# Four mixer layers and two feed-forwards on one core: the builder's context orders the instructions by its timeline simulation

## The chip, the cores and the metric

One core of one Trainium2 chip runs the kernel. The metric is the device time of one execution in microseconds. Of the kernel before there are three runs, 1022.75 to 1022.98 us, median 1022.92. The core's engines have streams of their own and run side by side: TensorE (PE in the profile, its weight loads PEld), VectorE (DVE), ScalarE (ACT), GpSimd (POOL) and the queue that issues transfers (SP).

## The reference

The input is 256 tokens of width 1024. Two blocks work on them. The first has two equal layers, each on a normalised `h`:

```python
(hq, hf, hi, hgo, hz, nq, kcm, vcm, ksl, vsl, kwn, vwn, ngate, nz) = split(rmsnorm(h) @ w_in[i])
y_hg  = rmsnorm(hgrn2_chunkwise(hq, log_f, k_hg, hi)) * sigmoid(hgo) * silu(hz)
kc    = rmsnorm(compress(kcm));  vc = compress(vcm)        # 15 compressed keys and values
o_nsa = gates[0] * o_cmp + gates[1] * o_slc + gates[2] * o_win
y_nsa = o_nsa * silu(nz)
h = h + concat([y_hg, y_nsa]) @ w_out[i]
h = h + sigmoid(rmsnorm(h) @ w_pg[i]) * (p[i] @ w_pp[i])
```

`hgrn2_chunkwise` is a gated linear recurrence over four heads, `o_cmp`, `o_slc` and `o_win` are eight-head softmax attentions over compressed, selected and windowed keys. The second block has an even layer (a recurrence and short convolutions), a feed-forward, an odd layer and another feed-forward, each added to `h`, with a norm at the end. The odd layer joins a spatial gating unit (gelu of a projection, normalised, mixed over tokens) and an eight-head softmax attention with a decay. A feed-forward is `(silu(gate) * val) @ w_down`, where gate and val come from a three-tap convolution of `x @ w_up` (2 x 2816 columns).

## The kernel before

The residual `h` is held in SBUF as two tiles of 128 tokens, and each layer works on all 256 tokens. Weights pass through once, in pieces of 128 x 1024. `wload` and `wgroup` issue the transfer of a piece (`raw`, three buffers); ScalarE makes the rounded part (`whi`, L262), VectorE the rest (`wlo`, L265), five buffers each. A product is three matmuls: high by high, high by low, low by high (`mm3`, L364). Helpers hold most instructions, so their lines repeat: L257 transfer, L262 ScalarE operation, L265 VectorE operation of two tensors, L364 matmul, L411 POOL.

`first_layer` (L566 to 815) does the first block's layers. From `h` it makes the normalised and transposed `xA` (`xT`, L430), then the projections: `F`, `hq`, `K`, `Q` (the queries `nq`), `hz`, `hgo` and `nz`. Between them run the recurrence, head by head, and from L719 on the queries' norm and transposes (`qT`). The compressed keys come from `compress` (L864 to 895): matmul `pkc`, its squares on ScalarE (`ksq`), sums on VectorE (`kv`), a root on POOL (`kr`), scaling on VectorE (`kc`), a transpose on TensorE (`kcT`). Scores `cs` (L364) give the weights `ce`, transposed as `cpt`.

`nsa` (L980 to 1031) does the selected and windowed attention in twelve blocks per layer, four for the first half of tokens and eight for the second. A block is: four or two matmuls `as` and a mask matmul `causal` into one of two accumulators; on VectorE the negated maximum `anm` (L1017); on ScalarE the exps `pr` with their sums; on VectorE the reciprocal (L1024), the gate and the multiplication of `pr` by `af`; on TensorE four transposes `apt` (L1030); on VectorE the copy `pts` (L1031). Two blocks' copies feed `no`. After the gate `yA` the output matmuls `po` add into `h`. `pp` is the product of `p` and `w_pp`, `pg` the gate of that last step.

In the odd layer `as`, `pr` and `fo` belong to the attention, `og` (gate side) and `ou` (other side) to the spatial gating. In a feed-forward `up` is the first product, `pd` the second, with four sums (two halves of tokens by two halves of columns). The last norm (`Last`, L494, L498) writes `fin`, which goes out by four transfers.

No table sets the order of instructions, and it isn't written by hand. `body` emits operations as the text has them, and the builder's context collects them, simulates when each could start, and puts out each engine's and queue's stream in the order which that simulation gives. Engines run their streams in that order; waits on other engines are put in by the context.

## Time and profile before

| what | value |
|---|---|
| median of three runs | 1022.92 us (1022.75 to 1022.98) |
| the profiled execution's own time | 1022.92 us |
| its span, first to last instruction | 1021.1 us |
| TensorE busy | 985.7 us, 97% of the span |
| TensorE weight loads | 869.6 us, 85% |
| VectorE busy | 806.4 us, 79% |
| ScalarE busy | 599.1 us, 59% |
| POOL busy | 35.3 us, 3% |
| read from memory | 164.30 MB, 162 GB/s over the span |
| chain that ended last | TensorE 74%, VectorE 10%, transfers 6%, ScalarE 4% |

The busy share says which engine has the most work, the chain which engine the end waited for, and the table by stretches whether this holds in each stage. A row of a timeline gives start, duration, engine, line, operation, output and inputs, and in brackets how long the engine had stood idle and what ended it. Matmuls overlap in TensorE's pipe, so the step from start to start is shorter than a single one's duration.

### The profile page before, as it was taken

What the parts mean: (1) busy time and instruction counts of PE and PEld (TensorE: products, weight loads), DVE (VectorE), ACT (ScalarE), POOL (GpSimd) and SP (SyncE); (2) the same over time, 40 slices, a digit from 0 to 9 for tenths busy, and PEclk for the clock granted to TensorE, in tenths of its full rate; (3) what the DMA queues carried; (4) which work ended last, traced back from release to release, by engine and by line L of the source; (5) the groups of instructions that cost most, each with busy time, mean ns of one, the idle gap of its engine ahead of it and who ended that gap; (6) DMA issues with size and microseconds to landing.
All of it is one profiled execution on the core that took longest, in us unless ns stands there. A gap on an engine that the chain in (4) does not pass through costs nothing.

```text
span 1021.1 us, 17129 instructions
## 1 busy us (share of the span) xinstructions
PE 985.7 (97%) x6524; PEld 869.6 (85%) x6524; DVE 806.4 (79%) x1439; ACT 599.1 (59%) x1061; POOL 35.3 (3%) x44
## 2 busy tenths in 40 slices
PE   7999899999998999999999999999989999999997
PEld 5879787778797786799889999998888899999995
DVE  5778889987878898778968877777667869777776
ACT  6753555577644654666657555555756556555553
POOL 1001100000002000000100000000000000000000
PEclk9999999999999999999999999999999999999999
DMA  8741543565503525555755766665582546666661
GB/s 295 240 145 53 146 147 115 192 197 157 186 15 112 179 63 174 169 164 160 236 181 150 222 186 186 186 186 177 166 227 62 175 143 203 186 186 188 186 186 57
DMA packets 48098, 168.03 MB, mean 165 GB/s; under 512 B 5648, under 2 KB 6672, under 8 KB 47376
## 3 DMA queue, kind: packets, MB, share of 16 engines
q1 hardware_dynamic: 48016, 166.94, 53.7%
q8 instruction: 51, 0.84, 0.3%
q14 instruction: 31, 0.25, 0.1%
HBM read 164.30 MB, written 1.05 MB: 162 GB/s over the span
## 4 chain that ended last, share of the span: by engine, by line
PE 74%; DVE 10%; DMA 6%; ACT 4%; issue 3%; POOL 2%; SPq 0%; POOLq 0%; ACTq 0%; DVEq 0%
PE up L364 25%; PE pd L364 12%; PE po L364 5%; DVE wlo L265 4%; PE pg L364 3%; PE pl L364 2%; PE hq L364 2%; PE nz L364 2%; PE hgo L364 2%; PE Q L364 2%; ACT whi L262 2%; PE as L364 2%; PE F L364 2%; DMA raw<-in_win_dram 2%; POOL hr L411 2%
## 5 line engine op out<-in xcount | busy, mean ns | idle before, releaser
L262 ACT ACTIVATE whi<-raw 128x1024 fp32r<-128x1024 f32 (+2 forms) x295 | 309.7, 1052 | 231.6 <-PE up L364 59.8
L265 DVE TENSOR_TENSOR wlo<-raw,whi 128x1024 fp32r<-128x1024 f32 (+2 forms) x295 | 356.8, 1212 | 91.9 <-ACT whi L262 88.8
L364 PE MATMUL pd<-whi,fhl 128*128 128x512 f32 x352 | 115.8, 391 | 0.0
L364 PE MATMUL up<-xFlo,whi 128*128 128x256 f32 x352 | 99.6, 283 | 0.5 <-DVE xFlo L435 0.5
L364 PE MATMUL up<-xDlo,whi 128*128 128x256 f32 x352 | 99.6, 283 | 0.5 <-DVE xDlo L435 0.5
L364 PE MATMUL up<-xDhi,whi 128*128 128x256 f32 x352 | 99.4, 283 | 0.2 <-ACT xDhi L262 0.2
L364 PE MATMUL up<-xFhi,whi 128*128 128x256 f32 x352 | 99.4, 283 | 0.2 <-ACT xFhi L262 0.2
L364 PE MATMUL up<-xFhi,wlo 128*128 128x256 f32 x352 | 99.5, 283 | 0.0
L364 PE MATMUL up<-xDhi,wlo 128*128 128x256 f32 x352 | 99.5, 283 | 0.0
L364 PEld LDWEIGHTS pd<-whi,fhl 128*128 128x128 f32 x352 | 66.2, 188 | 14.0 <-ACT fhl L262 0.9
L1047 DVE SCALAR_TENSOR_TENSOR fc<-fp,colp,fc 128x255 f32<-128x255 f32 (+1 forms) x176 | 73.5, 478 | 0.8 <-ACT fc L262 0.7
L364 PE MATMUL pd<-wlo,fhl 128*128 128x512 f32 x176 | 69.1, 392 | 0.0
L364 PEld LDWEIGHTS up<-xDlo,whi 128*128 128x128 f32 x352 | 67.5, 192 | 1.5 <-DVE xDlo L435 0.7
L364 PEld LDWEIGHTS up<-xFlo,whi 128*128 128x128 f32 x352 | 67.5, 192 | 1.5 <-DVE xFlo L435 0.7
L364 PEld LDWEIGHTS up<-xFhi,whi 128*128 128x128 f32 x352 | 67.3, 192 | 1.2 <-ACT xFhi L262 0.5
L364 PEld LDWEIGHTS up<-xDhi,whi 128*128 128x128 f32 x352 | 67.3, 192 | 1.2 <-ACT xDhi L262 0.5
L364 PEld LDWEIGHTS up<-xFhi,wlo 128*128 128x128 f32 x352 | 67.5, 192 | 0.0
L364 PEld LDWEIGHTS up<-xDhi,wlo 128*128 128x128 f32 x352 | 67.5, 192 | 0.0
L262 ACT ACTIVATE fc<-fp,colp 128x256 f32<-128x256 f32 x88 | 47.6, 586 | 2.5 <-DVE fp L265 2.4
L262 ACT ACTIVATE fhl<-fc 128x256 fp32r<-128x256 f32 x44 | 18.2, 414 | 44.9 <-DVE fc L265 44.9
L262 ACT ACTIVATE pr<-as,anm 128x128 f32<-128x128 f32 (+1 forms) x80 | 32.6, 423 | 17.8 <-PE apt L1030 6.7
L265 DVE TENSOR_TENSOR fp<-up,R 128x512 f32<-128x512 f32 x44 | 30.3, 690 | 15.9 <-PE up L364 15.8
(477 smaller groups left out, 2416.2 us busy)
## 6 DMA issues: line engine op xcount, KB each, us to landing
raw<-in_up_dram SPq DMA_DIRECT2D x88, 512.0 KB, 3.9
raw<-in_win_dram SPq DMA_DIRECT2D x64, 512.0 KB, 4.3
raw<-in_down_dram SPq DMA_DIRECT2D x44, 512.0 KB, 4.1
raw<-in_ein_dram SPq DMA_DIRECT2D x20, 512.0 KB, 4.1
raw<-in_oin_dram SPq DMA_DIRECT2D x20, 512.0 KB, 4.2
raw<-in_wout_dram SPq DMA_DIRECT2D x16, 512.0 KB, 3.7
raw<-in_wpg_dram SPq DMA_DIRECT2D x16, 512.0 KB, 4.0
cw<-in_cw_dram SPq DMA_DIRECT2D x4, 1024.0 KB, 6.9
```

The lines of the kernel that those rows point to most:

```text
L262: A.activation(o, i, f, **kw)
L265: V.tensor_tensor(o, x, y, op=op)
L364: PE.matmul(o, l, r, start=start, stop=stop)
L411: G.tensor_tensor(o, v, mh[:, :v.shape[1]], op=OP.pow)
L1047: V.scalar_tensor_tensor(dst[:, k:], src[:, :T - k], w, dst[:, k:], op0=OP.mult, op1=OP.add)
```

## The change

One argument is given to the builder's context. The operations, tiles and buffers are as they were; the simulation by which the streams are ordered is another.

```diff
     out = nc.dram_tensor("out_0_dram", (T, D), F32, kind="ExternalOutput").ap()
-    with tile.TileContext(nc) as tc:
+    with tile.TileContext(nc, schedule_with_timeline_sim=True) as tc:
         body(tc, aps, offs, out)
```

TensorE keeps its 6188 instructions and VectorE its 1441, SP and POOL theirs; ScalarE has 951 instead of 945, six more loads of an activation table. What moves is shown at three places.

TensorE, layer 0, in the attention blocks. `as_1317` is the third block of the layer, `apt` the transposes of earlier blocks. Before:

```order
L364 MATMUL nz_1693<-xA0hi_93,wlo_1697 128x256
L364 MATMUL nz_1693<-xA0hi_93,whi_1696 128x256
L364 MATMUL as_1317<-kA_412,qs_1131 128x2x128
L364 MATMUL as_1317<-kA_413,qs_1131 128x2x128
L364 MATMUL as_1317<-kA_412,qs_1131 128x2x128
L364 MATMUL as_1317<-kA_413,qs_1131 128x2x128
L364 LDWEIGHTS identb_82
L364 MATMUL as_1317<-causal_81,identb_82 128x512
L364 MATMUL no_1224<-ces_1245,VB_1202 128x512
L1030 MATMUL apt_1267<-ident_76,pr_1258 128x128 x4
L364 MATMUL nz_1693<-xA0lo_94,whi_1696 128x256
L364 MATMUL nz_1693<-xA0hi_93,wlo_1697 128x256
```

TensorE of the same layer with the change, from the start of the compressed keys on:

```order
L729 MATMUL qT_1180<-ident_76,q2_1170 128x128 x4
L364 MATMUL pkc_1186<-cw2_651,hT_649 32x64
L364 MATMUL pvc_1200<-cw2_651,rep_1198 128x64
L890 MATMUL kcT_1216<-ident_76,kc_1195 128x32
L364 MATMUL as_1273<-kA_412,qs_1131 128x2x128
L364 MATMUL as_1273<-kA_413,qs_1131 128x2x128
L364 MATMUL as_1273<-kA_412,qs_1131 128x2x128
L364 MATMUL as_1273<-kA_413,qs_1131 128x2x128
L364 LDWEIGHTS identb_82
L364 MATMUL as_1273<-causal_81,identb_82 128x512
L364 MATMUL cs_1225<-kcT_1218,qnT_945 128x32 x4
L364 MATMUL as_1295<-kA_412,qs_1131 128x2x128
```

And further on, at `as_1317`:

```order
L364 MATMUL as_1317<-kA_412,qs_1131 128x2x128
L364 MATMUL as_1317<-kA_413,qs_1131 128x2x128
L364 LDWEIGHTS identb_82
L364 MATMUL as_1317<-causal_81,identb_82 128x512
L364 MATMUL no_1224<-ces_1245,VB_1202 128x512
L1030 MATMUL apt_1267<-ident_76,pr_1258 128x128 x4
L1030 MATMUL apt_1289<-ident_76,pr_1280 128x128 x4
L364 MATMUL as_1370<-kA_412,qs_1173 128x512
```

Before, `hgo`, `nz` and `pp` matmuls stood between the links of the chain and between the blocks. With the change 48 `hgo`, 96 `nz`, 24 `pp` and 24 `po` stand ahead of `pkc`, and 42 `po` between the blocks; layer 1 has the same pattern.

ScalarE, odd layer, at the end of the attention blocks. Before:

```order
L262 ACTIVATE pr_8255,asum_8192<-as_8246,anm_8193 128x256 x2
L262 ACTIVATE pr_8277,asum_8192<-as_8268,anm_8193 128x256 x2
L262 ACTIVATE whi_8524<-raw_8522 128x1024
L262 ACT_TABLE_LOAD
L262 ACTIVATE og_8377<-og0_8327,r_7741 128x512
L262 ACTIVATE og_8400<-og1_8328,r_7741 128x512
L262 ACTIVATE yEhi_8116<-fo_8191 128x4x128
L262 ACTIVATE sq_8379<-og_8377 128x512
```

With the change:

```order
L262 ACTIVATE whi_8524<-raw_8522 128x1024
L262 ACT_TABLE_LOAD
L262 ACTIVATE pr_8136,asum_8119<-as_8121,anm_8120 128x128 x4
L262 ACT_TABLE_LOAD
L262 ACTIVATE og_8377<-og0_8327,r_7741 128x512
L262 ACT_TABLE_LOAD
L262 ACTIVATE pr_8166,asum_8119<-as_8151,anm_8120 128x128 x4
L262 ACT_TABLE_LOAD
L262 ACTIVATE og_8400<-og1_8328,r_7741 128x512
```

The gelus of `og` moved between the exps of the attention, with a load at each turn from one function to the other.

SP, the start of the program, behind the last transfer of `h`. Before:

```order
L257 DMA raw<-in_win_dram 128x1024
L257 DMA colp<-in_colp_dram 128x889
L257 DMA rowp<-in_rowp_dram 128x512
L257 DMA raw<-in_win_dram 128x1024 x2
L257 DMA stage<-in_c_stage_dram 128x2048
L257 DMA causraw<-in_c_causal_dram 128x128
L257 DMA raw<-in_win_dram 128x1024 x3
L257 DMA cw_651<-in_cw_dram 128x128
L257 DMA cw_653<-in_cw_dram 128x2048
```

With the change:

```order
L257 DMA colp<-in_colp_dram 128x889
L257 DMA rowp<-in_rowp_dram 128x512
L257 DMA stage<-in_c_stage_dram 128x2048
L257 DMA causraw<-in_c_causal_dram 128x128
L257 DMA cw_651<-in_cw_dram 128x128
L257 DMA cw_653<-in_cw_dram 128x2048
L257 DMA raw<-in_win_dram 128x1024 x3
L257 DMA cw_674<-in_cw_dram 128x2048
```

The weight pieces `raw` moved behind the constants and behind two pieces of the compression's weights (`cw`). At the end of the program the last matmuls of the four `pd` sums alternate, where each sum was finished before the next one.

## Rows read from the trace of the kernel before

**Rows 1.** The page, busy time and share of the span by engine.
```profile
PE 985.7 (97%) x6524; PEld 869.6 (85%) x6524; DVE 806.4 (79%) x1439; ACT 599.1 (59%) x1061; POOL 35.3 (3%) x44
```
**Rows 2.** Busy time by stretch: length, each engine's (instructions), granted clock, DMA share, GB/s.
```profile
0.00:25.00 25.00, 18.15 (x77) 14.40 (x78) 13.55 (x31) 16.43 (x34) 2.99 (x14) 1.00 0.87 295
...
62.00:113.00 51.00, 49.38 (x395) 43.69 (x394) 39.63 (x98) 22.78 (x40) 6.35 (x4) 1.00 0.24 71
...
135.00:181.00 46.00, 44.55 (x280) 34.38 (x279) 43.06 (x97) 28.99 (x85) 0.27 (x3) 1.00 0.34 110
...
535.00:706.00 171.00, 171.00 (x1233) 162.17 (x1232) 137.62 (x210) 99.64 (x146) 0.00 (x0) 1.00 0.63 185
...
730.00:797.00 67.00, 60.95 (x485) 54.87 (x485) 46.30 (x70) 40.20 (x74) 4.43 (x3) 1.00 0.53 152
...
831.00:1002.00 171.00, 171.00 (x1230) 162.16 (x1231) 137.68 (x211) 99.51 (x146) 0.00 (x0) 1.00 0.61 179
1002.00:1021.10 19.10, 11.78 (x53) 9.11 (x52) 10.44 (x22) 6.27 (x14) 1.10 (x2) 0.90 0.14 55
```
**Rows 3.** The chain that ended last, layer 0: start, duration, what.
```profile
132.17 5.79 PE hgo L364 x25
...
152.64 3.42 PE nz L364 x27
```
**Rows 4.** Tiles of layer 0: duration min/median/max in ns, first and last start in us.
```profile
L364 PE MATMUL Q<-whi,xA0hi x16: 387/396/502, 62.2 to 94.5; 128*128 128x512 f32 x16
...
L1017 DVE TENSOR_REDUCE anm<-as x12: 659/682/691, 135.3 to 169.8; 128x2 f32<-128x512 f32 x8, 128x4 f32<-128x512 f32 x4
...
L1031 DVE COPY pts<-apt x12: 679/688/692, 141.5 to 180.3; 128x512 f32<-128x512 f32 x12
...
L364 PE MATMUL po<-whi,yAlo x32: 387/389/497, 176.6 to 201.8; 128*128 128x512 f32 x32
```
**Rows 5.** Timeline of layer 0, compressed keys and first block.
```profile
124.05 0.30 PE L364 MATMUL pkc<-cw,hT 128*32 128x64 f32 x2
...
130.11 0.24 PE L890 MATMUL kcT<-ident,kc 32*128 32x32 f32 x1
...
135.33 0.68 DVE L1017 TENSOR_REDUCE anm<-as 128x4 f32<-128x512 f32 x1
```
**Rows 6.** VectorE's groups by form, 108 to 205 us: busy us, mean ns, idle before.
```profile
L265 DVE TENSOR_TENSOR wlo<-raw,whi 128x1024 fp32r<-128x1024 f32 x25 | 30.2, 1216 | 2.6 <-ACT whi L262 2.6
L265 DVE TENSOR_TENSOR pr<-pr,af 128x512 f32<-128x512 f32 x12 | 8.2, 682 | 0.0
...
L265 DVE TENSOR_TENSOR h<-po,h 128x512 f32<-128x512 f32 x4 | 2.7, 672 | 0.6 <-PE po L364 0.6
```
**Rows 7.** Start: SP's timeline, and busy time by stretch.
```profile
9.02 0.33 SPq L257 DMA_DIRECT2D raw<-in_win_dram  x1
...
17.00:21.00 4.00, 4.00 (x21) 3.24 (x20) 3.25 (x10) 3.15 (x6) 0.15 (x1) 1.00 0.98 331
```
**Rows 8.** ScalarE's timeline in the odd layer.
```profile
735.62 1.28 ACT L262 ACT_TABLE_LOAD   x1
736.92 0.42 ACT L262 ACTIVATE fe<-fe 8x256 f32<-8x256 f32 x1
```
**Rows 9.** The end: timeline, and busy time by stretch.
```profile
1013.22 5.08 SPq L257 DMA_DIRECT2D out_dram<-fin  x4
...
1015.35 0.69 DVE L265 TENSOR_TENSOR fin<-h,gfin 128x512 f32<-128x512 f32 x1 [0.24 <-DMA out_dram<-fin]
...
1014.50:1017.00 2.50, 0.00 (x0) 0.00 (x0) 1.56 (x6) 0.85 (x5) 0.55 (x1) 1.00 0.38 144
1017.00:1021.10 4.10, 0.00 (x0) 0.00 (x0) 0.46 (x1) 0.70 (x1) 0.00 (x0) 0.54 0.34 128
```
**Rows 10.** The chain that ended last, start of the program.
```profile
9.47 3.35 PE F L364 x7
...
17.47 5.99 PE F L364 x26
```

## Prediction, made before the result

> **What bounds the kernel now.** I read the engine totals first, then the busy time by stretch, then the tile rows of layer 0, and last single instructions. TensorE is busy 985.7 of 1021.1 us [rows 1], so at most 35.4 us is idle there. Both feed-forward stretches of 171 us are full to the last hundredth, 171.00 of 171 [rows 2]; VectorE has 137.62 and 137.68 in them and waits for TensorE. Those 342 us only give or take time if TensorE's own work changes, and it doesn't: both orders have the same matmuls. The other limit is in layers 0 and 1: while the selected-attention blocks run (135 to 181 us) VectorE is busy 43.06 of 46 and TensorE 44.55 [rows 2]. There a chain with many hands (matmul, VectorE maximum, ScalarE exp, VectorE scale, transposes, VectorE copy) runs beside dense projections that need no one's answer. Those projections keep TensorE at work while the chain turns. So the question is which matmuls stand beside the chain after the change.
>
> **Layers 0 and 1.** In the new order 48 `hgo`, 96 `nz`, 24 `pp` and the first 24 of 96 `po` matmuls stand ahead of `pkc`, the matmul that starts the compressed-key chain; before they stood behind it. Of `po` 42 more lie between the blocks; nothing else dense does. Price: 512 columns cost 5.79/25 = 0.232 us, the 256 columns of `nz` 3.42/27 = 0.127 us [rows 3]. So 96 x 0.232 + 96 x 0.127 = 34.5 us of cover goes ahead.
>
> The stretch from the first `Q` matmul (62.2) to the end of the last `po` (201.8 + 0.39 = 202.2) takes 140.0 us [rows 4]. For the new order I add it up anew:
> - First `Q` to `pkc`: 124.05 - 62.2 = 61.9 us before [rows 4, 5], plus 34.5, makes 96.4. TensorE idles about 1.6 us of 62 to 113 [rows 2], which the dense work standing ready could fill, and I take half as much again for 113 to 124: 96.4 - 2.4 = 94.0.
> - `pkc` to the first maximum `anm`: 135.33 - 124.05 = 11.3 us [rows 5]. The chain passes ScalarE, VectorE, POOL and VectorE before `kcT`, then goes on through `cs`. Until now `hgo` matmuls covered it. In the new order `kcT` stands directly behind `pvc`, so TensorE waits for it in order: 11.3 us bare.
> - First `anm` to the last copy `pts`: 45.7 us now (135.3 to 180.3 + 0.69) [rows 4]. VectorE must do per block a maximum, a copy [rows 4] and a multiply [rows 6], 0.682 + 0.688 + 0.682 = 2.05 us, 24.6 us for twelve blocks. TensorE's part is larger: of its 44.55 us there [rows 2] 92 `nz`, 24 `pp`, 12 `po` and some 13 `hgo` (until 137.96 [rows 3]) leave, 11.7 + 5.6 + 2.8 + 3.0 = 23.1, and 42 `po` come, 9.7: 31.2 us, the lower end. The weight subtractions between the blocks' steps (1.216 us each [rows 6]) move ahead, so 45.7 is the upper end. Only two accumulators serve the blocks and each engine waits for the other's answer, so I take 38, in the middle.
> - Last copy to last `po`: 30 `po` are left, 7.0 us, and the last outputs still have to be gated and transposed; by the present wait between copy 180.3 and the yet open `po` I give that 3.6 us: 10.6.
>
> 94.0 + 11.3 + 38 + 10.6 = 153.9 against 140.0: **+14 us per layer, +28 for two** (the second has the same order). With 31.2 the layer gives +7.1, with 45.7 it gives +21.6; both ends go into the range.
>
> VectorE's subtractions for that dense work must be done earlier too. VectorE has room, 39.63 us busy of 51 from 62 to 113 [rows 2]; I take nothing for them, and a lack of it is in the upper end.
>
> **Start.** SP now issues `colp`, `rowp`, `stage`, `causraw` and two of the `cw` transfers ahead of the fourth `raw` chunk, issued at 9.02 before [rows 7]. Together that is about 2.9 MB by shapes. At the 331 GB/s of 17 to 21 us [rows 7] these take 8.9 us and the chunk itself 1.6, so it lands near 20 and after two passes of about 1.2 us, copy and subtraction [rows 6], feeds `F` from 22.4 on; `F`'s last quarter (12 x 0.232 = 2.8) then ends at 25.2 instead of 23.5 [rows 10]. **+1.7 us**, between 0 (the bytes have to come anyway) and 4.
>
> **ScalarE in the odd layer.** Exp and gelu now alternate between the attention blocks, and the whole program has 21 table loads instead of 15. One takes 1.28 us; the next instruction begins at 736.92, 0.02 us after the load's end (735.62 + 1.28) [rows 8]. So 6 x 1.28 = 7.7 us more on ScalarE. TensorE idles 6 of the 67 us from 730 to 797 [rows 2]; in the new order `og` and `ou` matmuls stand between the blocks and can cover these idle times, while the exps wait for tables. I set both against each other: **0**, from -4 to +7.7. The Trainium skill (ScalarE: Activation LUTs, "What ACT_TABLE_LOAD costs") adds a drain and calls each switch about 2.66 us, an estimate of 16 us for six. By that page the sum would be 8 us higher; the rows here show the load alone and no drain behind it, so I keep 1.28.
>
> **Joints and tail.** Where the first feed-forward hands over to the odd layer, and that one to the second feed-forward, the sums now finish together instead of one after another, so the next normalisation starts later. The nearest row is the add into `h`, 0.672 us each [rows 6], three behind the first: **+2** at each joint (0 to 3). At the end of the kernel likewise: the four `pd` sums were finished one by one, and the first half's output went out from 1013.22 [rows 9]; now all four end within some 12 matmuls. VectorE then has four adds and four multiplies left (8 x about 0.69 = 5.5 us) where 1.56 + 0.46 = 2.0 us lay behind the last matmul, and the fourth `fin` buffer waits for an output transfer, which cost 0.24 us before [rows 9]. **+4**, from +2 to +6. Even layer and feed-forward: 0; their TensorE rows keep their pattern, and a full TensorE covers the rest.
>
> **Sum.** 28 + 1.7 + 0 + 2 + 2 + 4 = 37.7. The profiled execution took 1022.92 us, its span 1021.1 and 1.8 around it, and it is the median itself. 1022.9 + 37.7 = 1060.6, say **1061 us**. Lower ends together give 14 + 0 - 4 + 0 + 2 = 12, so 1035; upper ends 43 + 4 + 7.7 + 6 + 6 = 67, so 1090. All at one end at once is unlikely; half of the way to each gives 1048 to 1075.
>
> **Rivals.**
> *Faster, about 1008 (0.08).* Work standing ready earlier fills TensorE's idle time. Of its 35.4 us [rows 1] start and tail hold 14 (6.9 of the first 25 us, 7.3 of the last 19.1) [rows 2]; of the other 21 two thirds recovered is 14, so 1022.9 - 14 = 1009, and 1 less where the start gains as well. It decides at 35.4 us: if block stretch and chain together (45.7 + 11.3 now, the chain covered) take less than that, a layer falls below 140.0. For it: VectorE is freed exactly there, and TensorE's own part is only 31.2. Against it: the chain stands in TensorE's row with nothing of other kind between its links.
>
> *Nearly nothing, about 1027 (0.10).* With no subtractions and gates in the way every hand answers at once: the blocks run at TensorE's 31.2 us, and the chain takes its bare instructions; three of them take 0.30, 0.24 and 0.68 us [rows 5], so for the dozen I estimate 5.6, half of 11.3. A layer then costs 94.0 + 5.6 + 31.2 + 10.6 = 141.4, +1.4; the odd layer gains its 4, the joints cost nothing, start and tail 5.7: 1022.9 + 2.8 - 4 + 5.7 = 1027. VectorE's 43.06 of 46 speaks for it, since subtractions are what made that stretch full.
>
> *Much slower by the clock, about 1110 (0.04).* Seven 512-column matmuls of `F` took 3.35 us from 9.47 on, 0.48 each, and 26 took 5.99 us from 17.47 on, 0.23 each [rows 10]: TensorE's two levels, 1.2 and 2.4 GHz. In the last 4.1 us, behind the last matmul, the granted clock reads 0.54 [rows 9]. If the pauses between the bare blocks take the clock down, their 31.2 us of TensorE work become 62 instead of fitting into 38: +24 per layer, 1061 + 48 = 1109. Against it: from 730 to 797 us TensorE idles 6 of 67 and the granted clock stays at 1.00 [rows 2]. The Trainium skill (TensorE: Matmul & The Clock Gate, "What's actually happening") says it in general: throttled is the default, and activity releases it. No row here shows a stretch as thin as the new one.
>
> That the switch changes nothing is excluded by the two orders.
>
> **How the numbers follow.** Forecast 0.78, rivals 0.08, 0.10, 0.04. A difference below 0.2%, 2 us, can't be told from none. Faster than that is the first rival: 0.08. Within it falls some of the second's spread: 0.04. Slower: 0.88, mostly the forecast. For 8 in 10 the range takes the forecast's spread and the upper half of the second rival: 1028 to 1082. Below it lie the first rival and half of the second (0.13), above it the third and the forecast's worst (0.07).
>
> **What would show it.** Right: in layers 0 and 1 idle time of TensorE before `kcT`, `cs` and `apt`, released by VectorE and ScalarE, 8 to 20 us each; the stretch from first `Q` to last `po` near 154; both feed-forwards at 171 as before; the end after the last matmul near 10 us, where there were 6.6 (none from 1014.5 to 1021.1 [rows 9]). Wrong: if that stretch is under 140, the cover was not needed; if VectorE is full in it, the first part is limited by subtractions; if the granted clock falls below 1.00 there, the third rival holds.

## The result, and the profile after

The change takes 1105.88 us, median of four runs (1104.86 to 1108.4), against 1022.95 (1022.75 to 1026.13) for the kernel before: ratio 1.0808, 95% interval 1.0782 to 1.0834. The forecast was 1061, its range ended at 1082. The direction was right, the size less than half of the real one: +83 us instead of +38.

The profiled execution of the change took 1104.86 us, its span is 1103.0. Its page, totals and chain:

```profile
PE 1014.0 (92%) x6524; PEld 888.5 (81%) x6524; DVE 808.1 (73%) x1439; ACT 608.6 (55%) x1067; POOL 36.9 (3%) x44
...
PE 72%; DVE 13%; ACT 7%; DMA 3%; issue 3%; POOL 1%; SPq 0%; ACTq 0%; DVEq 0%; POOLq 0%
```

Against [rows 1] TensorE is busy 28.3 us longer with the same 6524 matmul records, and idle 89.0 us instead of 35.4. So there are two losses: idle time, and matmuls that take longer. The view by stretches (length, busy time and count of PE, PEld, DVE, ACT, POOL, granted clock, DMA share, GB/s) shows where:

```profile
0.00:26.50 26.50, 16.68 (x66) 12.31 (x67) 14.86 (x33) 16.20 (x33) 2.99 (x14) 1.00 0.90 326
64.80:169.20 104.40, 97.04 (x643) 84.91 (x643) 74.44 (x140) 48.26 (x69) 6.35 (x6) 0.97 0.42 123
169.20:177.10 7.90, 4.19 (x18) 3.46 (x18) 2.68 (x12) 1.26 (x5) 0.54 (x1) 0.69 0.52 183
177.10:223.00 45.90, 36.38 (x171) 24.08 (x172) 34.19 (x85) 18.19 (x74) 0.12 (x1) 0.87 0.06 24
223.00:234.00 11.00, 8.75 (x44) 5.77 (x42) 9.33 (x10) 4.84 (x6) 0.00 (x0) 1.00 0.55 191
...
92.00:96.00 4.00, 4.00 (x19) 3.90 (x18) 3.22 (x9) 1.23 (x2) 1.03 (x1) 0.50 0.03 12
...
176.00:180.00 4.00, 0.60 (x2) 0.60 (x3) 3.28 (x12) 2.46 (x14) 0.00 (x0) 0.50 0.00 0
208.00:212.00 4.00, 4.00 (x20) 2.16 (x19) 3.13 (x8) 1.94 (x8) 0.00 (x0) 0.50 0.00 0
600.00:778.00 178.00, 177.23 (x1280) 167.86 (x1280) 141.08 (x224) 104.18 (x160) 0.69 (x1) 1.00 0.63 186
800.00:881.00 81.00, 74.29 (x542) 66.58 (x540) 53.50 (x81) 54.88 (x93) 3.89 (x3) 0.98 0.56 156
904.00:1082.00 178.00, 177.60 (x1282) 168.40 (x1282) 140.63 (x229) 102.83 (x158) 0.69 (x1) 1.00 0.60 175
1082.00:1103.00 21.00, 10.18 (x45) 8.07 (x43) 8.89 (x21) 5.98 (x14) 1.10 (x2) 0.86 0.13 50
```

Both feed-forwards are nearly as full as before [rows 2]. In the four pieces of layer 0 (64.8 to 234.0) TensorE is busy 146.36 of 169.2 us, and the clock is at 0.50 for whole rows with TensorE at work. Layer 0's tiles, beside [rows 4, 5] (min/median/max ns, first and last start):

```profile
L364 PE MATMUL Q<-whi,xA0hi x16: 389/389/499, 64.8 to 77.6; 128*128 128x512 f32 x16
...
L364 PE MATMUL pkc<-cw,hT x2: 219/231/243, 169.2 to 169.3; 128*32 128x64 f32 x2
...
L1017 DVE TENSOR_REDUCE anm<-as x12: 680/684/692, 177.1 to 213.6; 128x2 f32<-128x512 f32 x8, 128x4 f32<-128x512 f32 x4
...
L1031 DVE COPY pts<-apt x12: 681/691/692, 184.1 to 222.3; 128x512 f32<-128x512 f32 x12
...
L364 PE MATMUL po<-whi,yAlo x32: 388/393/501, 160.3 to 233.5; 128*128 128x512 f32 x32
```

First `Q` to `pkc` takes 104.4 us (61.9 before), `pkc` to the first maximum 7.9 (11.3), the blocks to their last copy 45.9 (45.7), the rest to the last `po` 10.9 (21.2): 169.1 in place of 140.0.

From these views I make a ledger for TensorE: idle time is length less busy time; *slow* is busy time in rows of 1 us times (1 - granted clock), the half of a slow matmul's time that the full clock would have saved; *work* is the remainder. That a matmul takes nearly twice as long shows in TensorE's timeline, by the step from start to start, 0.43 us at 96 and 0.23 at 98:

```profile
96.15 0.63 PE L364 MATMUL hz<-whi,xA0lo 128*128 128x512 f32 x1
96.58 0.63 PE L364 MATMUL hz<-whi,xA0hi 128*128 128x512 f32 x1
...
98.22 0.39 PE L364 MATMUL hz<-whi,xA0hi 128*128 128x512 f32 x1
98.45 0.40 PE L364 MATMUL hz<-wlo,xA0hi 128*128 128x512 f32 x1
```

| stretch | before: us, idle | after: us | idle | slow | difference |
|---|---|---|---|---|---|
| start to first `Q` | 62.2, 8.5 | 64.8 | 11.2 | 0 | +2.6 |
| layer 0, `Q` to last `po` | 140.0, 4.3 | 169.1 | 22.7 | 9.4 | +29.1 |
| last `po` to layer 1's `Q` | 73.4, 1.2 | 82.4 | 6.8 | 1.7 | +9.0 |
| layer 1, `Q` to last `po` | 140.7, 4.9 | 167.5 | 22.0 | 8.9 | +26.8 |
| last `po` to first `up` | 111.7, 1.5 | 116.6 | 3.8 | 2.9 | +4.9 |
| two feed-forwards | 356.0, 1.6 | 353.6 | 0.8 | 0 | -2.4 |
| between them (odd layer) | 118.3, 6.1 | 127.0 | 10.8 | 1.5 | +8.7 |
| tail | 18.8, 7.3 | 22.0 | 10.8 | 0 | +3.2 |
| sum | 1021.1, 35.4 | 1103.0 | 88.9 | 24.4 | +81.9 |

By the column of the granted clock *slow* is zero in every stretch of the kernel before. At the start that is only a lack of records: the trace's clock records begin at 13.8 us (11.8 in the change), and until then matmuls last and step as in the slow rows above. Before:

```profile
10.07 0.63 PE L364 MATMUL F<-wlo,xA0hi 128*128 128x512 f32 x1
10.49 0.63 PE L364 MATMUL F<-whi,xA0lo 128*128 128x512 f32 x1
...
14.11 0.40 PE L364 MATMUL F<-wlo,xA0hi 128*128 128x512 f32 x1
```

TensorE is busy 7.0 us (before) and 4.8 us (after) up to the first record, so some 3 us of slow time are not counted in either kernel. The 81.9 us are 53.5 of idle time, 24.4 of slow matmuls and 4.0 of other busy time, which was not parted further.

### The profile page after: what moved, and what is told of

It is laid out like the page before. It is cut to its first block, busy times and chain, and to the rows that moved or that the text cites. A ratio compares the mean times of both kernels' runs of the same rounds, so it can differ in the third digit from the quotient of the medians.

```text
span 1103.0 us, 17167 instructions
## 1 busy us (share of the span) xinstructions
PE 1014.0 (92%) x6524; PEld 888.5 (81%) x6524; DVE 808.1 (73%) x1439; ACT 608.6 (55%) x1067; POOL 36.9 (3%) x44
## 4 chain that ended last, share of the span: by engine, by line
PE 72%; DVE 13%; ACT 7%; DMA 3%; issue 3%; POOL 1%; SPq 0%; ACTq 0%; DVEq 0%; POOLq 0%
PE up L364 23%; PE pd L364 11%; PE po L364 7%; DVE wlo L265 4%; PE pg L364 3%; ACT whi L262 2%; PE oq L364 2%; PE cpv L364 2%; PE Q L364 2%; PE hgo L364 2%; PE pl L364 2%; DMA raw<-in_win_dram 2%; PE as L364 2%; PE hz L364 2%; DVE E L265 1%
## 5 line engine op out<-in xcount | busy, mean ns | idle before, releaser
L364 PEld LDWEIGHTS pd<-whi,fhl 128*128 128x128 f32 x352 | 65.9, 188 | 12.7
L265 DVE TENSOR_TENSOR fp<-up,R 128x512 f32<-128x512 f32 x44 | 30.3, 690 | 11.8 <-PE up L364 11.8
L364 PEld LDWEIGHTS pd<-wlo,fhl 128*128 128x128 f32 x176 | 33.2, 189 | 5.5
```

Source lines behind the costliest of these rows:

```text
L265: V.tensor_tensor(o, x, y, op=op)
L364: PE.matmul(o, l, r, start=start, stop=stop)
```

## The experiments

Each is a single run beside one run of the kernel before, and those varied from 1020.75 to 1026.95 us. So small differences between totals say nothing, and stretches of the traces are compared instead. Streams were fixed by edges that only set an order, between neighbours of a table for an engine.

### Whose order costs

Five runs took streams from one kernel into the other. Each is the kernel before, with or without the flag, and this behind `body`, for the engines and layers named. The edges fix the named engines alone; the context still orders the others by its simulation, with these edges in it:

```diff
     with tile.TileContext(nc) as tc:
         body(tc, aps, offs, out)
+        for x, y in zip(table, table[1:]):
+            tc.add_manual_dep(have[y], x, link, reason="order")
```

Without the flag; TensorE's order of the change in layers 0 and 1:

> The builder's default simulation, but TensorE's stream in layers 0 and 1 held to the order that the change gives it; the other engines' orders are free. Theory A (TensorE's order is the cause: dense products run ahead and the attention stands without cover): the two layers lose what they lose in the change, from first Q to last po 29.1 and 26.8 us and some more behind it, so 1079 to 1091 us. Rival B (the orders on VectorE and ScalarE are the cause: subtractions and reciprocals in front of what TensorE waits for): 1023 to 1040 us, since those engines are still ordered by the default simulation.

With the flag; TensorE's order of before in layers 0 and 1:

> The change, but TensorE's stream in layers 0 and 1 held to the order of the kernel before. Theory A: the layers' loss goes, about 56 to 68 us of the 83, so 1037 to 1050 us, and the granted clock is back at 1.00 in both layers. Rival B: 1080 to 1105 us.

With the flag; there TensorE's and VectorE's order of before, and then ScalarE's too:

> The change, with both TensorE's and VectorE's stream of layers 0 and 1 held to the order of the kernel before. With TensorE's alone it took 1072.94 us; there Q to pkc was 13 and 11 us and the block stretch 3 to 7 us longer than before. Theory V (those 30 us are VectorE's order): 1036 to 1045 us. Rival S (ScalarE's order: copies and exps late): 1060 to 1074 us.

> The change, with the streams of TensorE, VectorE and ScalarE in layers 0 and 1 all in the order of the kernel before. Both layers should then take what they took before, and what is left is the start (2 to 4 us), the odd layer with its joints (6 to 9) and the tail (3): 1035 to 1040 us. A rival that the order of transfers on SP matters inside the layers: 1045 us or more.

Measured: 1110.36; 1072.94; 1053.02; 1037.34; only the last lies in a range stated for it. With TensorE's new order the kernel loses 86 us, more than by the whole change; with the old one put back the change gives back only 33 and keeps 50. These are not prices of one stream, because the others moved too: in the first run's layers 0 and 1 the longest sequence that ScalarE's 497 operations share with the kernel before is 390, with the change 469; in the second run, of VectorE's 711 operations 507 stand in the order of before and 496 in the new one. What can be read is the end of the row: with three engines back, both layers are at 140.9 and 140.0 us again. The layers' loss lies in the orders of TensorE, VectorE and ScalarE together; 15 us are left outside the layers (start, odd layer, tail).

With the flag; TensorE, VectorE and ScalarE of before through the whole program; SP's and POOL's streams are left to the simulation, and SP's first 18 transfers come in the order of the change:

> The change, with TensorE's, VectorE's and ScalarE's streams held to the order of the kernel before in the whole program; SP's and POOL's are as the timeline simulation puts them. The joints and the tail should then be as before, and only the start stays: 2.6 to 4.8 us, 1025 to 1028 us. Rival: the order of the constants on SP costs nothing, 1022 to 1024 us.

1029.25, just above the stated range: the layers, odd layer and tail are as before (within 1 us), the start costs 4.8 us up to the first `Q`. In its timeline of SP the three weight pieces come at 11.79, where one stood at 9.02 [rows 7]:

```profile
9.75 1.63 SPq L257 DMA_DIRECT2D cw<-in_cw_dram  x2
11.79 2.64 SPq L257 DMA_DIRECT2D raw<-in_win_dram  x3
```

### What in TensorE's order costs

Without the flag; TensorE's order of before up to `pkc`, then the block of moved dense matmuls, then the change's order from `pkc` on, in both layers:

```diff
 qT x4
+hgo x48, nz x96, pp x24, po x24
 pkc
-pkc to the last po: order of before, hgo, nz, pp, po between the links
+pkc to the last po: order of the change
```

> The default simulation, but in layers 0 and 1 those 201 and 203 instructions stand in one block ahead of pkc, and what follows pkc has the changed order; the recurrence keeps the order of before. Theory A1: per layer 62 + 34.5 + 8 + 44 + 11 = 160 us from first Q to last po instead of 140, so +40 and some us behind it: 1060 to 1075 us. Rival A2: 1035 to 1050 us.

1088.87, above both ranges stated. For TensorE this is the prediction's own picture; the other streams followed by the simulation (of VectorE's 705 operations in both layers 592 stand in the order of before, of ScalarE's 497 only 416). Tiles of layer 0:

```profile
L364 PE MATMUL pkc<-cw,hT x2: 219/231/243, 160.4 to 160.5; 128*32 128x64 f32 x2
...
L1017 DVE TENSOR_REDUCE anm<-as x12: 671/683/693, 170.1 to 209.6; 128x2 f32<-128x512 f32 x8, 128x4 f32<-128x512 f32 x4
...
L1031 DVE COPY pts<-apt x12: 680/691/692, 178.3 to 218.3; 128x512 f32<-128x512 f32 x12
```

`Q` (at 62.1) to `pkc` is 98.3 us: 61.9 and the moved 34.5, and 1.9. Behind `pkc` only 8.7 us come back: 9.7 to the first maximum (11.3), 48.9 for the blocks (45.7), 10.9 at the end (21.2). Ledger of the blocks: 31.7 of work, 12.6 idle, 4.6 slow. **Bare of cover the blocks take as long as with it.**

The opposite edit keeps the flag and the change's order up to `pkc`:

```diff
-hgo x48, nz x96, pp x24, po x24
 pkc
-pkc to the last po: order of the change
+pkc to the last po: order of before, hgo, nz, pp, po between the links
```

> The change, but in layers 0 and 1 the 201 and 203 TensorE instructions (hgo, nz, pp, the first po and their transposes) that it moves ahead of pkc stand behind pkc again, in the order of before; the recurrence ahead of pkc keeps the changed order. Theory A1 (the lost cover of the attention is nearly all): like the order put back wholly, 1037 to 1055 us. Rival A2 (the changed order of the recurrence itself costs as much: Q to pkc took 104.4 us where 96.4 were reckoned): 8 us or more per layer stay, 1055 to 1075 us.

1093.27, above both ranges again, and just 12.6 us gained. `Q` to `pkc` falls from 104.4 to 82.9, not to 70, and the part behind it grows from 64.8 to 84.2. The ledger has the loss ahead of `pkc` now, 13.6 us idle and 9.9 slow, while the blocks, with cover between them, show no slow time and 4.7 idle. That the other streams deliver in an order which doesn't fit this one is likely, but not shown.

### The blocks: order inside TensorE's stream

In the change `po` and `no` stand ahead of the transposes `apt`. While ScalarE waits for those, it runs empty. The waits of 169 to 234 us (engine and line, whom it waited for: us, times, longest), ScalarE's and TensorE's own:

```profile
ACT pr L262 <- PE apt L1030: 19.4, 5, 6.6
...
PE as L364 <- ACT pr L262: 8.1, 5, 3.8
...
PE apt L1030 <- DVE pr L265: 1.9, 3, 1.4
```

The next run pulls each block's `apt` ahead, and puts `po` behind in sixes; another also moves VectorE's operations on `lb` in layer 0 behind the subtraction of a `wpg` piece. TensorE's row from the seventh block on:

```diff
 as x3, block 7
+apt x4, block 5
 as x3, block 8
+apt x4, block 6
-po x12
+po x6
 no
-apt x8, blocks 5 and 6
```

> The change, but inside the block stretch of layers 0 and 1 each block's apt stands right behind the as of the next but one block, and the po matmuls behind them in sixes, where in the change two apt stood behind 12 po. Theory Q (ScalarE's 37 us of waiting for apt is work queued ahead on TensorE, and with it the block stretch keeps 45 us): the stretch falls to 36 to 41 us, 1088 to 1098 us in all. Rival C (the chain's own length): 1100 to 1107 us.

> The kernel with the transposes unblocked (1102.63 us), and in layer 0 VectorE's six lb operations for layer 1 (7 us, 3.35 of them one reciprocal), which stand ahead of the last subtractions of weights, held behind the subtraction of a wpg piece. Theory L (they are what the last po and pg wait for once the block stretch is short): 6 to 8 us less, 1094 to 1097 us. Rival: the weights come late anyway, 1101 to 1104 us.

1102.63 and 1102.09, 3 to 4 us under the change's median and so hardly a gain, with a clearly shorter block stretch. Tiles and ScalarE's waits before `pr` in the first of them:

```profile
L1031 DVE COPY pts<-apt x12: 681/684/694, 183.9 to 216.6; 128x512 f32<-128x512 f32 x12
...
L364 PE MATMUL po<-whi,yAlo x32: 388/395/628, 160.4 to 234.5; 128*128 128x512 f32 x32
...
  PE apt L1030: 8.0, 3
```

From the first maximum (177.4) to the last copy it is 39.9 us instead of 45.9, and that wait falls from 19.4 to 8.0 us; but the last `po` comes at 234.5, where the change has it at 233.5. The ledger tells why: work in the blocks fell from 31.7 to 26.5, work behind them rose from 8.8 to 13.1, idle time of both went from 11.7 to 11.5, and slow from 4.7 to 6.5. The shorter stretch only left `po` for later. Weights come late at the end too: in SP's timeline of the change two issues of `cw` span 171.64 to 212.83 us, and the next weight piece goes out at 222.39; SP's own waits (165 to 236 us) say what held them, first `pts`, up to 212.5, and then a weight subtraction for 9.5 us:

```profile
171.64 41.19 SPq L257 DMA_DIRECT2D cw<-in_cw_dram  x2
222.39 2.06 SPq L257 DMA_DIRECT2D raw<-in_wpg_dram  x2
```

```profile
SPq L257 <- DVE pts L1031: 36.8, 1, 36.8
SPq L257 <- DVE wlo L265: 27.0, 4, 9.5
```

Whether the transfers' order matters by itself, asks the flag with SP's order of before in both layers, and nothing else fixed:

> The change, with SP's queue in layers 0 and 1 held to the order of the kernel before. In the change SP waits 41 us with two cw transfers of the next layer (171.6 to 212.8) while the pieces of wpg stand behind them, and hardly any byte moves from 177 to 205. Theory Z (this blocked queue makes the weights late behind the attention): 1090 to 1098 us, pg starts within 3 us of the last po. Rival W (the five weight buffers are held by po pieces whose matmuls wait for the attention, so nothing could be loaded anyway): 1102 to 1107 us.

1112.59, no gain and above both ranges: in layer 0 `Q` to `pkc` falls to 92.5, blocks and end grow to 52.5 and 17.0. TensorE's stream moved with it (of 2570 matmuls in both layers 2301 stand in the order of the change), so this is no clean test of the transfers' order; it shows that putting that order back does not bring the layers back.

### Idle time ahead of `pkc`, and the clock

In the change TensorE stands 2.49 us before a `kT`, then the clock is at 0.50 from 91 to 97 us. VectorE has the operation `kd`, which `kT` needs, behind eight others. First I put twelve `hz` matmuls into that gap, and in a second run also the 24 `po` that stand ahead of `pkc` into the gaps of the compressed keys' chain (TensorE's row, both layers):

```diff
+hz x12
 kT x4
 pl x12
-hz x12
...
-po x24
 qT x8
+po x5
 qT x4
+po x3
 pkc
+po x7
 pvc
+po x2
 kcT, as x5, cs x4
+po x7
 as x5
```

> The change, with one difference in TensorE's order of layers 0 and 1: twelve hz matmuls, which stood behind the second half's kT and its pl, stand ahead of that kT. The same work, so it fills the idle time of 2.49 us before kT (88.4 to 90.9 us) with 12 x 0.23 = 2.7 us that is owed anyway. In the changed kernel the granted clock is 0.50 behind that idle time, from 91 to 97 us, and the slower matmuls there make 3.1 us. Theory that the clock has a price on the path: the clock stays at 1.00 there, the stretch from first Q to pkc falls from 104.4 by 2.5 of idle time and 3.1 of slow matmuls, to about 99 in each layer, and the whole to about 1094. Rival, that the idle time alone has a price: the clock still falls, 102 in each layer and 1100. Second rival, that VectorE and ScalarE set the length of this stretch: still 104, the idle time comes back at pl or later, 1105.

> The one before, and also the 24 po matmuls that stood ahead of the last queries' transposes moved into the gaps of the compressed keys' chain: 5 and 3 of them ahead of the last transposes and pkc, 7 between pkc and pvc, 2 between pvc and kcT, 7 ahead of the third block's as, where TensorE waited 3.83 us for the exps. Theory that cover in TensorE's order is what the change lost: the stretch from first Q to pkc falls by another 24 x 0.232 = 5.6 us, pkc to the first maximum grows by at most 1 or even shrinks (as and cs at full clock), the rest as it is: some 6 us per layer against the run before, near 1082. Rival, that the blocks and the weights set the end: the last po stays where it was, as when apt was moved, and the whole gains under 2 us.

1120.96 and 1125.13. All three theories missed: `hz` had to wait 5.76 us for VectorE's `qn`, and `kT` behind it. In order, a matmul that looks ready on paper can be the next blocker. So the second attempt moved the 0.29 us on VectorE instead, and no matmul; its neighbour added the `po` moves:

```diff
 L265 TENSOR_TENSOR rA<-kd,colp 128x128
 L265 TENSOR_TENSOR rB<-kd,colp 128x8x8 x2
+L265 TENSOR_TENSOR kd<-rA,rB 128x8x16
 L265 TENSOR_TENSOR E_769<-E_769,hkT 128x64x4
...
 L520 TENSOR_REDUCE hss<-sq 128x8
-L265 TENSOR_TENSOR kd<-rA,rB 128x8x16
```

> The change with one VectorE operation of 0.29 us moved in each of layers 0 and 1: the sum kd of the second half, for which TensorE's kT waits 2.49 us, stands directly behind its own inputs rA and rB, no longer behind six products E, Ktop and a sum hss. All other streams of these layers are those of the change. No transfer and no matmul is moved. Theory that the lower clock has a price on the path: with the idle time gone the granted clock stays at 1.00 behind kT, the stretch from first Q to pkc loses 2.5 us of idle time and 3.1 of slow matmuls in each layer, 104.4 to about 99, and the whole comes to about 1094. Rival, only idle time has a price: the clock falls anyway or its loss lies beside VectorE's chain, 102 in each layer and 1100. Second rival, pl and the head's chain on VectorE set the length: 104 and 1105.

> The one before in its VectorE piece, and the 24 po matmuls ahead of the last queries' transposes moved into the gaps of the compressed keys' chain, as in the run that was lost to hz waiting for its accumulator. Theory that cover in TensorE's row is what was lost: from first Q to pkc another 4 to 5.6 us less in each layer than in the run beside it, pkc to the first maximum no more than 1 us longer with the granted clock at 1.00 in it (0.69 in the change), the rest as it is: 8 to 10 us less than the run beside it, about 1085. Rival, that it is given back: the blocks or the last po stretch by as much, and the two runs differ by less than 2 us.

1106.6 and 1109.59. TensorE's timeline of the first:

```profile
87.98 0.61 PE L684 MATMUL kT<-ident,kd 128*128 128x128 f32 x4
91.10 2.37 PE L364 MATMUL pl<-E 128*128 128x64 f32 x16 [2.52 <-DVE hv L522]
```

`kT` no longer waits, and `pl` waits 2.52 us in its place; the clock falls as before. The second rival was right: VectorE's chain sets this stretch, and the idle time moves to the next link. In the other run 4.1 us of `po` left the stretch ahead of `pkc`, which stayed at 104.9 (105.1 in the run beside it): idle time grew by 1.9 and slow by 1.9. Given back again: the whole took 3.0 us more than the run beside it. In the chain itself, though, cover did what it should. `pkc` to the first maximum, the run without and the run with `po` in the gaps:

```profile
169.60:177.80 8.20, 4.53 (x18) 3.73 (x18) 2.67 (x12) 1.26 (x5) 0.54 (x1) 0.59 0.47 171
```

```profile
169.10:178.10 9.00, 6.54 (x34) 4.75 (x34) 4.97 (x14) 3.27 (x7) 0.54 (x1) 0.98 0.28 76
```

By the ledger 4.1 us of work were added for 0.8 us: idle time fell by 1.2, slow from 2.1 to nothing. What stands on the path shows in the maximum `cm` of the scores `cs`, again without and with `po`:

```profile
176.31 0.29 DVE L980 TENSOR_REDUCE cm<-cs 128x8 f32<-128x128 f32 x1 [2.47 <-PE cs L364]
```

```profile
174.03 0.29 DVE L980 TENSOR_REDUCE cm<-cs 128x8 f32<-128x128 f32 x1 [0.92 <-PE cs L364]
```

It starts 6.7 us behind `pkc` without the `po` and 5.0 us with them, since the matmuls from the first `as` to the last `cs` take 1.8 us instead of 3.2. So here the lower clock had a price on the path, 1.7 us in this layer and 1.5 in the next. Behind `cm` the gain is lost: with `po` in the gaps, two weight subtractions of 1.23 us stand on VectorE ahead of the first maximum.

An earlier try to price the clock put 72 matmuls per layer into the gaps of chain and blocks, into accumulators that the next `as` or `apt` begins anew:

```diff
+                if H == 0 and j0 == 0 and par == 1:
+                    fill("as", 16, p4[:, :, 0, :], qs[:, 0], kks2[0][:, 0, :, :nk])
                 for h in range(hb):
...
+                if par == 1:
+                    fill("apt", ((2, 6, 6, 2)[j0] if H else (8 if j0 else 28)), pf[:, :, 0, :], qs[:, 0], kks2[0][:, 0, :, :nk])
                 for i in range(4):
```

> The change, with 72 matmuls per layer added behind pkc and between the blocks, where TensorE waits (they write into accumulators that the next real matmul overwrites, and add nothing to the result; about 11 us of work at the full clock, in about 13 us of idle time). Theory K (the clock's fall in the stretch costs 4 to 8 us per layer): granted clock 1.00 from pkc to the last copy, and 1089 to 1102 us. Rival N (the chain decides, the clock costs nothing there): 1103 to 1112 us with the clock at 1.00.

1116.97: chain and blocks grew by 5 and 7 us in the two layers, slow of layer 0 only fell from 9.4 to 8.7, and the whole lies above both ranges. It decides nothing: the fillers lengthened what they were to cover.

### The odd layer

Without the flag; ScalarE's order of the change in the odd layer, so 21 table loads:

> The default simulation, with ScalarE's stream from the odd layer's start to the first blocks of the second feed-forward held to the order of the change: 21 table loads instead of 15, exp and gelu alternating between the attention blocks; the other engines are free. Prediction's reading (the loads are covered by og and ou): 1021 to 1025 us. Rival T (each load is on the chain of the blocks): 7.7 us more, 1029 to 1033 us; with a drain behind each load 1037 us or more.

1040.99, +15.7 us in that layer (from the first feed-forward's last `up` to the second's first). The attention's output `fo`:

```profile
L364 PE MATMUL fo<-pts,ovs x48: 272/273/323, 792.4 to 813.1; 128*64 128x128 f32 x48
```

From its first to its last start 20.7 us, before 774.3 to 786.2, 11.9; in the change 865.8 to 879.7, 13.9. Six loads are 7.7 us. The remaining 8 were not parted further. `fo`'s longer span fits a wait for exps that come in another order, but the other engines were ordered anew around ScalarE's stream here too (of TensorE's 602 matmuls in this layer 452 stand in the order of before). With all streams new the layer loses 8.7, joints included.

## Why the prediction was wrong, step by step

**Layers, +28 forecast, +55.9 measured.** This is the step that failed: TensorE's work was added up correctly, the idle time and the slow time beside it were not. Of layer 0:

| step | forecast | measured | work | idle | slow |
|---|---|---|---|---|---|
| `Q` to `pkc` | 94.0 | 104.4 | 93.9 | 7.3 | 3.1 |
| `pkc` to first maximum | 11.3 | 7.9 | 2.5 | 3.7 | 1.6 |
| blocks to last copy | 38 | 45.9 | 31.7 | 9.5 | 4.7 |
| to last `po` | 10.6 | 10.9 | 8.8 | 2.2 | 0 |

- *"the dense work standing ready could fill"* the idle time of the first part: this failed. 94.0 was the work alone. Idle time there more than doubled (2.9 to 7.3) and 3.1 us of slow time came in. The orders of VectorE and ScalarE have a part in it: with only TensorE's order put back this stretch still took 75.0 us in place of 61.9, with VectorE's too 65.9, with ScalarE's too 62.8. And a gap closed at one link opened at the next (the `kd` run). Moved work costs its full length, 34.5 us, as the run with that block ahead of `pkc` showed (98.3).
- *"11.3 us bare"*: the chain takes 7.9 when nothing stands between its links; 3.4 too much. Before, TensorE was busy through all of the 11.3 us, so they were the length of the cover and not of the chain.
- *"I take 38, in the middle"*: the work of 31.2 was right (31.7), the answers' time was not. The upper end, 45.7, came true, not from VectorE's subtractions, as I had argued, but from idle time in TensorE's in-order stream and from the clock. The waits that I named stood elsewhere: TensorE waited 8.1 us for the exps ahead of `as`, 1.9 ahead of `apt`. And no middle value would have helped: the run that brought the stretch to 39.9 paid it back behind it.
- *"10.6"* held.

**No term at all** stood for the stretches from `po` to the next layer's `Q` and to the first `up`: +9.0 and +4.9, a third of the miss. I had said "even layer and feed-forward: 0" and gone over the step behind `po` without a row. Part of it is the weights: in the chain of waits a piece of `wpg` takes 3.69 us from 234.69 on, with nothing beside it.

**Start, +1.7; measured +2.6.** The mechanism held: the last `F` matmul starts at 26.3 us in place of 23.1. With the other engines' orders as before SP's costs 4.8; with all streams new it is 2.6.

**Odd layer and joints, 0 + 4; measured 8.7 - 2.4 with the feed-forwards.** 6.3, in the range. The first `oq` starts 4.3 us later behind the last `up` (+2 forecast). One load still takes 1.28 us, the next operation starts 0.02 us behind it (851.81 to 853.11 in the change). So no drain as the Trainium skill has it (ScalarE: Activation LUTs, "What ACT_TABLE_LOAD costs"); that the run with ScalarE's order cost 15.7, close to the estimate of 16 by that page, is a coincidence and no drain, since in that run too the next operation starts 0.02 us behind a load.

**Tail, +4; measured +3.2.** Right, and for the reason named. VectorE's timeline has the adds together and the wait for the output transfer, 2.16 us instead of 0.24 [rows 9]:

```profile
1090.86 1.89 DVE L265 TENSOR_TENSOR h<-pd,h 128x512 f32<-128x512 f32 x3 [4.94 <-PE pd L364]
...
1098.78 0.69 DVE L265 TENSOR_TENSOR fin<-h,gfin 128x512 f32<-128x512 f32 x1 [2.16 <-DMA out_dram<-fin]
```

**Rivals.** The first two were wrong: idle time was not filled but more than doubled. The third named 1110, near the measured time; that is partly luck, since its mechanism gives 24.4 us here, not 48. The clock does fall to 0.50, 1.2 GHz, in the bare stretches, as that rival and my sign for it said. The slow `F` at the start [rows 10] was sound evidence: its matmuls last 0.63 us, as at 0.50, and the 1.00 in the column stands where no clock was recorded. The argument against it, from the odd layer, was too weak: the 6 us there lie in pieces of 1.3 us at most, while in the change the clock falls after waits such as the 2.49 us before `kT`. The length of one wait doesn't settle it: in the odd layer of the change a wait of 2.25 us that ends at 861.9 is followed by 0.50, one of 2.33 that ends at 835.4 is not. That the clock falls back agrees with the Trainium skill (TensorE: Matmul & The Clock Gate, "What's actually happening"), that throttled is the default. How much of the 24.4 lies on the path stays open: 1.7 and 1.5 us were shown in the chains of the two layers; elsewhere the two losses could not be parted, since what closed a gap moved it.

## What to carry to other kernels

Independent matmuls in front of a chain of many engines cost their full length (34.5 us of them cost 36.4, and 8.7 came back); between its links they cost little (4.1 us for 0.8). So price a reordering by what still covers each link, stretch by stretch, with idle time, slow time and work apart. Streams of in-order engines go together as a set: holding one engine to another order made the context move the others, so such a run is not the price of one stream, and it can cost more than the whole change. A gap closed at one link can show up at the next one. A stretch that gets shorter is a gain only when the work in it got no less.

## What the runs showed of the hardware

The granted clock can fall within a single wait: after 2.49 us before `kT` it reads 0.50 from 91 to 97 us with TensorE fully busy, and a 512-column matmul steps 0.43 us instead of 0.23. In the kernel before, with cover between the links, no stretch from the first clock record (13.8 us) to the last matmul shows a granted clock below 1.00; in the changed one up to 24.4 us of busy time are due to it. Where a trace has no clock record the column reads 1.00 all the same: up to 13.8 us the matmuls last 0.63 us, as at 0.50. A wait in SP's stream holds all that stands behind it: 36.8 us for one VectorE copy, `pts`, then 9.5 us for a weight subtraction, and no weight piece goes out from 168.85 to 222.39 us.
